# The w_down stage of a decoder layer by Strassen's seven block products

## The chip, the cores and the metric

One Trainium2 chip, one core of it. TensorE multiplies, VectorE and ScalarE work on tiles, GpSimd is nearly unused, and SyncE (SP) issues the DMA transfers. The metric is the time of one execution on the device in microseconds; before the change 788.14 (median of 3 runs, 787.05 to 790.59).

## The reference, cut to what matters

One decoder layer in float32: 512 tokens of width 1024. A normalised and modulated input goes through two attention branches, their outputs through gates and an output projection into a residual; then follows the SwiGLU block, of width 2816, that the change is about:

```python
h = rms_norm(x, g_ffn_norm[l]) * (1.0 + sc_f) + sh_f
g_ff, u_ff = jnp.split(h @ w_gate_up[l], 2, axis=-1)
x = x + gt_f * ((jax.nn.silu(g_ff) * u_ff) @ w_down[l])
```

`gt_f`, the output gate, is a row of 1024 numbers made from `c` and `w_mod`. It multiplies each output column.

## The kernel before, in words

Every large product is done in three passes (`mm3`). Each operand is split into a high part (ScalarE casts it to the fast matmul format) and a low part (VectorE subtracts the high part from the original); the passes are high x high, high x low, low x high, added up in one PSUM bank. So a weight tile passes through SP (load into one of three staging tiles `st`), ScalarE (`wh`) and VectorE (`wl`) before TensorE can use it; `wh` and `wl` have three buffers each.

The work is a list of chunks, run in order by `drive`. A chunk is 256 weight rows by 512 columns; `prep(c + 2)` is started when chunk c has begun: it takes the loaded staging tile, has it split, and issues the load of the chunk after. All other work beside the matmuls (splitting of activations, rows of gates, normalisation) is a set of generators, called tasks. A planner with a modelled clock for each engine (`Clocks`) decides while the program is written where their instructions go: `step` lets a task go on when what it yields is ready on that clock, `pump` moves TensorE's modelled clock on where something is missing, and `need_room` and `room` wait for a free buffer of a tag. Each engine then runs its instructions in the order in which they were written; nothing is reordered on the chip.

The up stage makes, for each of 11 groups `gi`, 256 features: four 128-feature blocks (two of the gate part, two of the up part) in four PSUM banks. `up_done` takes Silu of the gate part on ScalarE into a tile `s`, multiplies the up part into it on VectorE, and a task `up_split` makes high and low parts, which stay in SBUF: `g` tiles for groups 0 to 3, `K` for 4 to 7, `O` for 8 to 10. Even groups use the `acc` banks, odd ones the banks `s`, `tr`, `tr`, `pv`. The normalised input `h2` lies in the four `H` tiles.

The last stage, w_down, runs once for each half of the 1024 output columns: 11 chunks of 256 rows, for each 128-row block k and token tile i (128 tokens) one `mm3` into the bank of that token tile. Before a chunk's weights are split, `gated` multiplies them by `gt_f` on VectorE. At the end `add_store` adds the bank to the residual `x1` and SP stores the sum. In the second half `down_end` runs the last chunk's part of the last token tile in two pieces of 256 columns, each with its own bank, add and store:

```python
def gated(half):
    def change(st):
        pump(lambda: "gtf" in ready)
        ve.tensor_tensor(out=st, in0=st, in1=gtf[half].unsqueeze(1).to_broadcast([P, 2, 512]), op=ALU.mult)
```

Of the kernel before, what the change touches and what calls it, by code (L numbers as in the profile page):

```python
# [24 lines left out]
P = 128  # L26
# [87 lines left out]
def layer(ctx, tc, x, vecs, w_mod, w_in, gvecs, w_br_dsa, w_br_moba, w_out, w_gate_up, w_down, cosh, sinh, cosi, sini, out):  # L114
# [48 lines left out]
    def mm3(acc, lh, ll, rh, rl, first, last):  # L163
        te.matmul(acc, lh, rh, start=first, stop=False)
        te.matmul(acc, lh, rl, start=False, stop=False)
        te.matmul(acc, ll, rh, start=False, stop=last)
# [385 lines left out]
    def group(srcs, n, accs_of, mm, order, fin, need=(), change=None, end=None):  # L552

        accs = {}
        nk = 2 * len(srcs)
        chunks = []
        for c, src in enumerate(srcs):
            def unit(w, ks, js, last, c=c):
                if not accs:
                    accs.update(accs_of())  # L560

                held_back[0] = 1.0 if last else 0.0
                pieces = [(k, j) for j in js for k in ks] if last else [(k, j) for k in ks for j in js]
                if end and last and js[-1] == order[-1]:
                    del pieces[-len(ks):]
                for a, b in pieces:

                    full = nk - 2 if end and b == order[-1] else nk

                    emptied_next[0] = last and a == ks[-1]  # L570
                    mm(accs[b], w[0][:, a], w[1][:, a], 2 * c + a, b, c == 0 and a == 0, 2 * c + a == full - 1)
                    if end and b == order[-1] and 2 * c + a == full - 1:
                        fin(b, accs[b], False)
                        done(accs[b])
# [5 lines left out]
                if end and last and js[-1] == order[-1]:  # L580
                    end(w, [2 * c + a for a in ks])
# [5 lines left out]
            chunks.append((lambda src=src, n=n: wload(src, 2, n), units, need, change))  # L587
        return chunks

    def drive(chunks, ws, ahead=2):  # L590
# [6 lines left out]

        def prep(c):
            if c < len(chunks) and chunks[c][0]:
                yield lambda: 0.0 if c in sts else None  # L600
                st = sts.pop(c)
                if chunks[c][3]:
                    chunks[c][3](st)
                yield st
                uid[0] += 1
                h, l = [wp.tile(list(st.shape), F32R, name=f"w{q}_{uid[0]}", tag="w" + q) for q in "hl"]
                se.copy(h, st)
                yield h
                ve.tensor_tensor(out=l, in0=st, in1=h.bitcast(F32), op=ALU.subtract)
                done(st)  # L610
                ws[c] = h, l
            load(c + 1)

        load(ahead)
        for c, (load_of, units, need, _) in enumerate(chunks):
            pump(lambda: all(f in ready for f in need) and (not load_of or c in ws))
            for u, unit in enumerate(units):
                unit(ws.get(c))
                if u == 0:
                    spawn(prep(c + ahead), slack=4.0, rank=-1, on=(DVE,))  # L620
                    step()
            ws.pop(c, None)
# [604 lines left out]
    act = []  # L1227

    def up_split(src, hi, lo):
        f = f"act{len(act)}"  # L1230
        act.append((hi, lo))
        yield src
        se.copy(hi, src)
        yield hi
        ve.tensor_tensor(out=lo, in0=src, in1=hi.bitcast(F32), op=ALU.subtract)
        done(src)
        ready.add(f)

    def up_done(gi):
        half = {}  # L1240

        def fin(f, acc):
# [6 lines left out]
            if gi < 4:  # L1249
                need_room("g")  # L1250
                need_room("g")
                dst = t("g", [P, S], F32R), t("g", [P, S], F32R)
            else:
                if not f:
                    need_room("K" if gi < 8 else "O")
                    half["big"] = t("K" if gi < 8 else "O", [P, 4, S], F32R)
                dst = half["big"][:, 2 * f, :], half["big"][:, 2 * f + 1, :]
# [47 lines left out]

    gtf = []
# [12 lines left out]
    def down_mm(acc, wh, wl, k, i, first, last):  # L1319
        sl = slice(i * P, (i + 1) * P)  # L1320
        pump(lambda: f"act{k}" in ready)
        main3(acc, act[k][0][:, sl], act[k][1][:, sl], wh, wl, first, last)

    def gated(half):
        def change(st):
            pump(lambda: "gtf" in ready)
            ve.tensor_tensor(out=st, in0=st, in1=gtf[half].unsqueeze(1).to_broadcast([P, 2, 512]), op=ALU.mult)
        return change

    def add_store(i, cols, part, store=True):  # L1330
# [5 lines left out]
    def down_done(half):  # L1336
        return lambda i, acc, store=True: add_store(i, slice(half * 512, half * 512 + 512), acc, store)

    def down_end(w, ks):

        sl = slice((NT - 1) * P, NT * P)
        for a, tag in ((0, "pv"), (256, "s")):
            need_room("ps" + tag)
            part = ps(tag, (P, 256))
            cs = slice(a, a + 256)
            for n, k in enumerate(ks):
                mm3(part, act[k][0][:, sl], act[k][1][:, sl], w[0][:, n, cs], w[1][:, n, cs], n == 0, n == len(ks) - 1)
            add_store(NT - 1, slice(512 + a, 768 + a), part)
            done(part)

    for half in range(2):
        hs = slice(half * 512, half * 512 + 512)
        chunks += group([[w_down[k2 * 256:(k2 + 1) * 256, hs]] for k2 in range(NF // 2)], 512,
                        four() if half else other_four, down_mm, [0, 1, 2, 3], down_done(half), change=gated(half),
                        end=down_end if half else None)

    with tc.manual_schedule(engines=engines):
        start = max(ck.at.values())
        ck.at = {e: start for e in engines}
        free.update({tag: [start] * n for tag, n in list(NB.items()) + [("st", 3)]})  # L1360
# [23 lines left out]
        spawn(gtf_task())  # L1384
        dve = (DVE,)
# [48 lines left out]
```

## Time and profile before

| | before |
|---|---|
| median of 3 runs | 788.14 us |
| the profiled execution | 790.77 us |
| its span, first to last instruction | 788.7 us |
| mean granted TensorE clock | 0.993 |
| TensorE / VectorE / ScalarE / GpSimd busy | 780.8 / 478.3 / 363.4 / 30.4 us |
| DMA | 100.61 MB, mean 128 GB/s |

The rows come from one profiled execution. A busy TensorE is not one at its peak, since matmuls overlap: a row's mean duration of a matmul is longer than the distance to the next. What a matmul costs is read from a run of them in the chain of waits, as time over count.

### The profile page before, as it was taken

The numbers are of one execution on the slowest core, as the hardware profiler recorded it, in microseconds if no ns is written. First come the engines' busy times: TensorE is split into PE (matmuls) and PEld (weight loads), VectorE is DVE, ScalarE is ACT, GpSimd is POOL, SyncE is SP. The second block draws the span as 40 slices with busy tenths as digits, with TensorE's granted clock in tenths as the row PEclk, the third lists the DMA queues.
The fourth block names the chain that finished last, engine by engine and source line by source line (L and its number), as shares of the span: only waits on it lengthen the run. The fifth ranks groups of instructions, "written<-read, shape, count | busy, mean of one in ns | idle before, by whom it ended". The sixth has DMA issues, their size and how long they took to land.

```text
span 788.7 us, 10060 instructions
## 1 busy us (share of the span) xinstructions
PE 780.8 (99%) x3734; PEld 649.7 (82%) x3734; DVE 478.3 (61%) x876; ACT 363.4 (46%) x767; POOL 30.4 (4%) x32
## 2 busy tenths in 40 slices
PE   7999999999999999999999999999999999999998
PEld 6887888888788878888889988888888888888886
DVE  5874889989799786248777365323333334544542
ACT  5664587779776747624446132222332332211210
POOL 2000012011111000000000000000000000000000
PEclk8999999999999999999999999999999999999999
DMA  9957443542136364334520166333233232333311
GB/s 302 334 173 225 129 162 81 150 141 58 31 88 200 111 213 152 118 106 146 165 90 27 56 200 207 98 107 107 85 104 107 81 105 62 127 107 113 128 54 53
DMA packets 80156, 100.61 MB, mean 128 GB/s; under 512 B 8096, under 2 KB 48360, under 8 KB 80108
## 3 DMA queue, kind: packets, MB, share of 16 engines
q1 hardware_dynamic: 80108, 99.98, 40.7%
q8 instruction: 29, 0.48, 0.2%
q14 instruction: 19, 0.16, 0.1%
HBM read 97.86 MB, written 2.11 MB: 127 GB/s over the span
## 4 chain that ended last, share of the span: by engine, by line
PE 98%; DMA 1%; ACT 0%; SPq 0%; issue 0%; DVE 0%; ACTq 0%
PE psacc L107 64%; PE pstr L107 16%; PE pspv L107 9%; PE pss L107 9%; DMA K<-in_w_mod_dram 1%; SPq L218 0%; ACT H L107 0%; SPq L202 0%; DVE V L107 0%; ACT acol L107 0%; DVE mcol L107 0%; ACT mcol L107 0%; DVE acol L107 0%; ACTq L107 0%
## 5 line engine op out<-in xcount | busy, mean ns | idle before, releaser
L107 DVE TENSOR_TENSOR wl<-st,wh 128x1024 fp32r<-128x1024 f32 (+1 forms) x120 | 145.1, 1209 | 134.8 <-ACT wh L107 134.8
L107 ACT CAST wh<-st 128x1024 fp32r<-128x1024 f32 (+1 forms) x120 | 124.4, 1037 | 172.8 <-PE psacc L107 62.1
L107 PE MATMUL psacc<-H,wh 128*128 128x512 f32 x576 | 183.0, 399 | 0.0
L107 PE MATMUL psacc<-wh,H 128*128 128x512 f32 x384 | 127.3, 403 | 0.3 <-ACT H L107 0.2
L107 PEld LDWEIGHTS psacc<-H,wh 128*128 128x128 f32 x576 | 106.2, 188 | 22.3 <-issue 2.1
L107 PE MATMUL psacc<-H,wl 128*128 128x512 f32 x288 | 112.6, 391 | 0.0
L107 PEld LDWEIGHTS psacc<-wh,H 128*128 128x128 f32 x384 | 72.7, 190 | 16.1 <-ACT H L107 1.1
L107 PE MATMUL psacc<-wl,H 128*128 128x512 f32 x192 | 72.0, 396 | 0.0
L107 PEld LDWEIGHTS psacc<-H,wl 128*128 128x128 f32 x288 | 54.1, 188 | 11.6
L107 PE MATMUL pstr<-H,wh 128*128 128x512 f32 (+1 forms) x176 | 54.3, 390 | 0.0
L107 POOL TENSOR_TENSOR m<-m,mhalf 128x4 f32<-128x4 f32 (+1 forms) x24 | 28.6, 1191 | 394.9 <-DVE m L107 360.9
L107 PEld LDWEIGHTS psacc<-wl,H 128*128 128x128 f32 x192 | 36.8, 192 | 7.0
L107 PE MATMUL psacc<-wh,K 128*128 128x512 f32 x128 | 39.8, 390 | 0.0
L107 PE MATMUL psacc<-O,wh 128*128 128x512 f32 x128 | 39.5, 390 | 0.0
L107 PEld LDWEIGHTS pstr<-H,wh 128*128 128x128 f32 (+1 forms) x176 | 32.3, 184 | 7.6
L107 ACT ACTIVATE s<-s,att 128x256 f32<-128x256 f32 (+3 forms) x64 | 34.2, 562 | 4.0 <-DVE att L107 3.8
L107 DVE TENSOR_TENSOR s<-psacc,s 128x512 f32<-128x512 f32 x12 | 8.3, 692 | 43.7 <-PE psacc L107 43.7
L107 PE MATMUL pstr<-H,wl 128*128 128x512 f32 (+1 forms) x88 | 34.3, 390 | 0.0
L107 ACT ACTIVATE s<-psacc 128x512 f32<-128x512 f32 x12 | 7.2, 598 | 47.6 <-PE psacc L107 47.6
L107 PEld LDWEIGHTS psacc<-wh,K 128*128 128x128 f32 x128 | 24.0, 188 | 5.0
L107 PEld LDWEIGHTS psacc<-O,wh 128*128 128x128 f32 x128 | 24.0, 188 | 5.0
L107 DVE TENSOR_TENSOR st<-st,cg 128x1024 f32<-128x1024 f32 x22 | 26.8, 1219 | 0.0
(236 smaller groups left out, 1362.9 us busy)
## 6 DMA issues: line engine op xcount, KB each, us to landing
st<-in_w_gate_up_dram SPq DMA_DIRECT2D x88, 256.0 KB, 3.2
st<-in_w_in_dram SPq DMA_DIRECT2D x36, 512.0 KB, 3.6
K<-in_w_mod_dram SPq DMA_DIRECT2D x12, 1024.0 KB, 6.7
st<-in_w_down_dram SPq DMA_DIRECT2D x22, 512.0 KB, 3.6
K<-in_w_mod_dram SPq DMA_DIRECT2D x16, 512.0 KB, 6.1
st<-in_w_in_dram SPq DMA_DIRECT2D x16, 256.0 KB, 4.7
st<-in_w_mod_dram SPq DMA_DIRECT2D x8, 512.0 KB, 3.7
O<-in_x_dram SPq DMA_DIRECT2D x4, 512.0 KB, 5.3
```

What stands on the lines that cost most here:

```text
L107: inst = f(*args, **kw)
```

## The change: what it does

The last stage is computed as a 2 x 2 block product. Tokens are halved (256 each), the features of every group are halved (128-row blocks 2c and 2c + 1 of w_down), and the output columns are halved (512 each). Instead of eight block products there are seven, M1 to M7, each over 11 pairs of row blocks and two token tiles. Their operands are blocks and sums of blocks: S1 to S4 of the activations and T1 to T4 of the weights, made on VectorE in float32 before the split into high and low parts.

- After each up group a task `combine` makes S1 to S4. A11, S2, S1 and S3 stay in SBUF (`g`, `K`, `O` tiles as before). A12, A22 and S4 go, split, into an `O` tile and from there to device memory by a transfer on GpSimd's queue (`second0` to `second10`, 768 KB each).
- The stage has two halves. The first runs M1, M6, M7 and M5 for pairs 0 to 10, with B11 and T1 to T3 of each pair, from 768 KB of w_down; B11 + T3, that is T2, is also stored to device memory (256 KB, GpSimd's queue). The second runs M2, M3 and M4 with B21, B22 and T4, from 512 KB of w_down and the 256 KB stored. `second_task` loads the second activations back into `K` and `O` tiles as these come free.
- Split weights live in three sets (`homes`): one in four of the six `wh` and `wl` buffers, two in the `H` tiles, which the last up group leaves in two steps. Second blocks `b` of a load use `pT` tiles, and `gu` tiles after the last group's activations are stored. Preparation begins three chunks ahead.
- M2 goes on in M1's banks. At the first half's end `shared_sums` copies M1 and makes the sums from which three of the four output quarters start; `share` gates them and adds them to `x1`. The gate no longer multiplies weights: `settle` multiplies each product's bank by `gt_f` and then adds it.
- The last two chunks of the second half run together, product by product; the last one (M4, second token tile) takes them in two pieces of 256 columns.

```diff
         def prep(c):
+            early = c < len(chunks) and chunks[c][3]
+            def load_next():
+                if c + 1 < len(chunks) and chunks[c + 1][3]:
+                    yield room("st"), lambda: block_room()
+                load(c + 1)
             if c < len(chunks) and chunks[c][0]:
                 yield lambda: 0.0 if c in sts else None
+                if early:
+                    yield from load_next()
+                ws[c] = yield from (chunks[c][3] or split)(sts.pop(c))
+            if not early:
+                yield from load_next()
+        begun = [ahead]
+        def prepare(c):
+            while begun[0] <= c + (ahead + 1 if begun[0] < len(chunks) and chunks[begun[0]][3] else ahead):
+                spawn(prep(begun[0]), slack=4.0, rank=-1, on=(DVE,))
+                begun[0] += 1
...
+    def combine(gi, a0, a1):
+        first, other = slice(0, 256), slice(256, 512)
+        yield a0, a1, room("gu", 2)
+        s13, s4 = t("gu", [P, 2, 256]), t("gu", [P, 256])
+        ve.tensor_tensor(out=s13[:, 0], in0=a0[:, other], in1=a1[:, other], op=ALU.add)
+        ve.tensor_tensor(out=s13[:, 1], in0=a0[:, first], in1=a0[:, other], op=ALU.subtract)
+        ve.tensor_tensor(out=a0[:, other], in0=s13[:, 0], in1=a0[:, first], op=ALU.subtract)
+        ve.tensor_tensor(out=s4, in0=a1[:, first], in1=a0[:, other], op=ALU.subtract)
+        if gi < 4:
...
+        va = a0.rearrange("p (a d) -> p a d", a=2)
+        se.copy(ha, va)
+        se.copy(hb, s13)
+        yield ha, hb
+        ve.tensor_tensor(out=la, in0=va, in1=ha.bitcast(F32), op=ALU.subtract)
+        ve.tensor_tensor(out=lb, in0=s13, in1=hb.bitcast(F32), op=ALU.subtract)
+        done(a0, s13)
...
+        yield s4, a1, room("O")
+        v1 = a1.rearrange("p (a d) -> p a d", a=2)
+        x = t("O", [P, 6, 256], F32R)
+        se.copy(x[:, 0:2], v1)
+        se.copy(x[:, 2], s4)
+        yield x
+        ve.tensor_tensor(out=x[:, 3:5], in0=v1, in1=x[:, 0:2].bitcast(F32), op=ALU.subtract)
+        ve.tensor_tensor(out=x[:, 5], in0=s4, in1=x[:, 2].bitcast(F32), op=ALU.subtract)
+        done(a1, s4)
+        second_acts[gi] = dp.tile([P, 6, 256], F32R, name=f"second{gi}")
+        pool_dma(second_acts[gi], x, out_of=x)
+        done(x)
+        ready.add(f"stored{gi}")
...
             ve.tensor_tensor(out=half[f], in0=acc, in1=half[f], op=ALU.mult)
-            spawn(up_split(half[f], *dst), rank=0)
-            step()
-            if gi == 0 and f:
+            if f and not gi:
                 done(*w0_tiles)
                 ready.add("ffn0")
+            if f:
+                spawn(combine(gi, half[0], half[1]), rank=0)
+            if f and gi == NF // 2 - 1:
+                done(h2[1], h2[3])
+            step()
...
+    last_up = chunks[-2][1]
+    last_up[0] = lambda w, unit=last_up[0]: (done(h2[0], h2[2]), unit(w))
...
+    def homes(n):
+        sets[0] += 1
+        uid[0] += 1
+        if sets[0] % 3 == 1:
+            yield room("W")
+            parts = [wp.tile([P, 2, 512], F32R, name=f"w{q}{m}_{uid[0]}", tag="w" + q) for m in range(2) for q in "hl"]
+            taken("W", parts[0])
+            return [(parts[0], parts[1]), (parts[2], parts[3])], parts[:1]
+        yield room("H", 2)
+        h, l = t("H", [P, n, 512], F32R), t("H", [P, n, 512], F32R)
+        return [(h[:, 0:2], l[:, 0:2]), (h[:, 2:], l[:, 2:])], (h, l)
...
+    def split_into(places, blocks):
+        yield tuple(b for b, _ in blocks)
+        for (b, view), (h, l) in zip(blocks, places):
+            se.copy(h, view)
+        yield tuple(h for h, _ in places)
+        for (b, view), (h, l) in zip(blocks, places):
+            ve.tensor_tensor(out=l, in0=view, in1=h.bitcast(F32), op=ALU.subtract)
...
+    def block_tag():
+        tags = [tag for tag in ("pT", "gu") if free[tag] and (tag == "pT" or f"stored{NPAIR - 1}" in ready)]
+        return min(tags, key=lambda tag: min(free[tag]), default=None)
...
+    def load_first_half(c):
+        st, b = rows_of(2 * c), t(block_tag(), [P, 512])
+        last_dma[0] = nc.sync.dma_start(b, w_down[(2 * c + 1) * P:(2 * c + 2) * P, 512:])
+        arriving(b, 512)
+        return c, st, b
+    def split_first_half(loaded):
+        c, st, b = loaded
+        yield st, b, room("s")
+        t2 = t("s", [P, 512])
+        ve.tensor_tensor(out=b, in0=b, in1=st[:, 1], op=ALU.subtract)
+        ve.tensor_tensor(out=t2, in0=b, in1=st[:, 0], op=ALU.add)
+        ve.tensor_tensor(out=st[:, 1], in0=st[:, 1], in1=st[:, 0], op=ALU.subtract)
+        sums2[c] = dp.tile([P, 512], F32, name=f"sums{c}")
+        places, tiles = yield from homes(4)
+        (h0, l0), (h1, l1) = places
+        places = [(h0, l0), (h1[:, 0], l1[:, 0]), (h1[:, 1], l1[:, 1])]
+        yield from split_into(places, [(st, st), (b, b), (t2, t2)])
+        pool_dma(sums2[c], t2, out_of=t2)
+        done(st, b, t2)
+        return {"B11": (h0[:, 0], l0[:, 0]), "T1": (h0[:, 1], l0[:, 1]), "T3": places[1], "T2": places[2]}, tiles
...
+    def load_second_half(c):
+        st, b = rows_of(2 * c + 1), t(block_tag(), [P, 512])
...
+    def split_second_half(loaded):
+        c, st, b = loaded
+        yield st, b
+        ve.tensor_tensor(out=b, in0=st[:, 0], in1=b, op=ALU.subtract)
+        places, tiles = yield from homes(3)
+        (h0, l0), (h1, l1) = places
+        places = [(h0, l0), (h1[:, 0], l1[:, 0])]
+        yield from split_into(places, [(st, st), (b, b)])
+        done(st, b)
+        return {"B21": (h0[:, 0], l0[:, 0]), "B22": (h0[:, 1], l0[:, 1]), "T4": places[1]}, tiles
...
+    def second_task():
+        for q in range(NPAIR):
+            yield (f"stored{NPAIR - 1}", "down",
+                   lambda: min([min(free[tag]) for tag in ("K", "O") if free[tag]], default=None))
+            tag = min((tag for tag in ("K", "O") if free[tag]), key=lambda tag: min(free[tag]))
+            x = t(tag, [P, 6, 256], F32R)
+            pool_dma(x, second_acts[q])
...
+    def settle(i, half, acc, cs=slice(0, 512), store=True):
+        pump(lambda: "gtf" in ready)
+        need_room("s")
+        tmp = t("s", [P, 512])
+        n = cs.stop - cs.start
+        ve.tensor_tensor(out=tmp[:, :n], in0=acc[:, :n], in1=gtf[half][:, cs], op=ALU.mult)
+        cols = slice(half * 512 + cs.start, half * 512 + cs.stop)
         xs = x1[i // 2][:, i % 2, cols]
-        ve.tensor_tensor(out=xs, in0=xs, in1=part, op=ALU.add)
+        ve.tensor_tensor(out=xs, in0=xs, in1=tmp[:, :n], op=ALU.add)
+        done(tmp)
         if store:
             nc.sync.dma_start(ov[:, i, cols], xs)
...
+    def shared_sums(n, tt, acc):
+        if n == "M1":
+            kept["M1", tt] = fresh()
+            se.copy(kept["M1", tt], acc)
+        elif n == "M6":
+            kept["U2", tt] = fresh()
+            ve.tensor_tensor(out=kept["U2", tt], in0=acc, in1=kept["M1", tt], op=ALU.add)
+            done(kept["M1", tt])
+        elif n == "M7":
+            kept["U3", tt] = fresh()
+            ve.tensor_tensor(out=kept["U3", tt], in0=acc, in1=kept["U2", tt], op=ALU.add)
+        else:
+            c22, c12 = fresh(), fresh()
+            ve.tensor_tensor(out=c12, in0=acc, in1=kept["U2", tt], op=ALU.add)
+            ve.tensor_tensor(out=c22, in0=acc, in1=kept["U3", tt], op=ALU.add)
+            done(kept["U2", tt])
+            spawn(share(tt, c12, c22, kept["U3", tt]), slack=1.0, rank=3, on=(DVE,))
+    def share(tt, c12, c22, u3):
+        yield "gtf"
+        for i, half, c in ((2 + tt, 1, c22), (tt, 1, c12), (2 + tt, 0, u3)):
+            yield c
+            ve.tensor_tensor(out=c, in0=c, in1=gtf[half], op=ALU.mult)
...
+            ve.tensor_tensor(out=xs, in0=xs, in1=c, op=ALU.add)
+            done(c)
+            if c is c22:
+                nc.sync.dma_start(ov[:, i, 512:], xs)
...
+    first_half = [("M1", "A11", "B11", ("tr", "tr")), ("M6", "S2", "T2", ("pv", "s")),
+                  ("M7", "S3", "T3", ("acc", "acc")), ("M5", "S1", "T1", ("acc", "acc"))]
+    second_half = [("M2", "A12", "B21", None), ("M3", "S4", "B22", ("pv", "s")), ("M4", "A22", "T4", ("acc", "acc"))]
...
+        def part(w, rows):
+            begin(w)
+            held_back[0] = 0.0 if second or c < last else 1.0
+            for n, a, b, tags in rows:
+                for tt in range(2):
...
+                    ends = c == last if not second else c == last - 2 and (n, tt) == ("M4", 1)
+                    product(n, a, b, tt, c, held, ends, acc, start=not c and n != "M2", skip=n == "M2")
+                    if ends:
+                        emptied_next[0] = False
+                        finish(n, tt)
+                        step()
+            if rows[-1] is table[-1]:
+                leave(c)
+        def end(w):
+            begin(w)
+            held_back[0] = 1.0
+            for n, a, b, tags in table:
+                for tt in range(2):
+                    if (n, tt) == ("M4", 1):
+                        continue
+                    for q in (last - 1, last):
+                        emptied_next[0] = q == last
+                        product(n, a, b, tt, q, held, q == last, banks[n, tt], skip=n == "M2")
+                    emptied_next[0] = False
+                    finish(n, tt)
+                    step()
+            n, a, b, _ = table[-1]
+            for e, tag in ((0, "pv"), (256, "s")):
+                need_room("ps" + tag)
+                acc = ps(tag, (P, 256))
+                cs = slice(e, e + 256)
+                for q in (last - 1, last):
+                    product(n, a, b, 1, q, held, q == last, acc, cs=cs, start=q != last, more=False)
+                settle(3, 0, acc, cs=cs)
+                done(acc)
+            leave(last - 1, last)
+        return [lambda w: part(w, table[:2]), lambda w: part(w, table[2:])]
```

## Rows read from the trace of the kernel before

**Rows 1.** The page's busy shares and granted clock in 40 slices.

```profile
PE 780.8 (99%) x3734; PEld 649.7 (82%) x3734; DVE 478.3 (61%) x876; ACT 363.4 (46%) x767; POOL 30.4 (4%) x32
...
PEclk8999999999999999999999999999999999999999
```

**Rows 2.** The page's chain of waits, shares of the span by engine.

```profile
PE 98%; DMA 1%; ACT 0%; SPq 0%; issue 0%; DVE 0%; ACTq 0%
```

**Rows 3.** Windows: stretch, each engine's busy us (instructions), clock, DMA share, GB/s.

```profile
443.70:643.70 200.00, 200.00 (x898) 166.22 (x897) 81.05 (x93) 59.66 (x77) 0.00 (x0) 1.00 0.38 116
...
665.60:725.60 60.00, 60.00 (x267) 49.71 (x266) 29.75 (x28) 12.83 (x14) 0.00 (x0) 1.00 0.33 106
725.60:785.60 60.00, 59.98 (x271) 49.76 (x269) 26.25 (x25) 9.85 (x10) 0.00 (x0) 1.00 0.23 79
```

**Rows 4.** Chain of waits from 720 us: start, us, engine, tile.

```profile
725.67 58.48 PE psacc L107 x258
784.15 0.71 PE pspv L107 x6
784.86 0.73 PE pss L107 x6
785.62 0.42 DVE V L107
```

**Rows 5.** VectorE's groups by shape from 665.6 us: count, busy us, mean ns, idle.

```profile
L107 DVE TENSOR_TENSOR wl<-st,wh 128x1024 fp32r<-128x1024 f32 x21 | 25.7, 1225 | 47.4 <-ACT wh L107 47.4
L107 DVE TENSOR_TENSOR st<-st,cg 128x1024 f32<-128x1024 f32 x20 | 24.4, 1219 | 0.0
...
L107 DVE TENSOR_TENSOR O<-s,O 128x512 fp32r<-128x512 f32 x2 | 1.4, 683 | 0.0
```

**Rows 6.** VectorE's timeline, 663 to 673 us: start, duration, idle before.

```profile
663.22 0.69 DVE L107 TENSOR_TENSOR s<-psacc,s 128x512 f32<-128x512 f32 x1 [6.10 <-PE psacc L107]
663.83 1.22 DVE L107 TENSOR_TENSOR st<-st,cg 128x1024 f32<-128x1024 f32 x1
...
667.14 1.22 DVE L107 TENSOR_TENSOR wl<-st,wh 128x1024 fp32r<-128x1024 f32 x1
668.28 0.69 DVE L107 TENSOR_TENSOR O<-s,O 128x512 fp32r<-128x512 f32 x1
668.88 1.22 DVE L107 TENSOR_TENSOR st<-st,cg 128x1024 f32<-128x1024 f32 x1
671.29 1.22 DVE L107 TENSOR_TENSOR wl<-st,wh 128x1024 fp32r<-128x1024 f32 x1 [1.19 <-ACT wh L107]
672.44 1.22 DVE L107 TENSOR_TENSOR st<-st,cg 128x1024 f32<-128x1024 f32 x1
```

**Rows 7.** ScalarE's timeline, 654 to 667 us.

```profile
654.80 1.05 ACT L107 CAST wh<-st 128x1024 fp32r<-128x1024 f32 x1 [4.39 <-PE psacc L107]
661.79 0.60 ACT L107 ACTIVATE s<-psacc 128x512 f32<-128x512 f32 x1 [5.93 <-PE psacc L107]
...
666.66 0.62 ACT L107 CAST O<-s 128x512 fp32r<-128x512 f32 x1
```

**Rows 8.** DMA issues (us to landing); two busy windows, the last columns share, GB/s.

```profile
st<-in_w_down_dram SPq DMA_DIRECT2D x22, 512.0 KB, 3.6
...
20.00:40.00 20.00, 19.82 (x93) 16.27 (x92) 17.26 (x35) 13.63 (x26) 0.00 (x0) 0.92 1.08 333
460.00:480.00 20.00, 20.00 (x90) 16.54 (x89) 12.11 (x16) 6.33 (x9) 0.00 (x0) 1.00 0.64 202
```

**Rows 9.** VectorE's timeline at the end.

```profile
784.19 0.69 DVE L107 TENSOR_TENSOR V<-V,psacc 128x512 f32<-128x512 f32 x1 [0.67 <-PE psacc L107]
784.90 0.42 DVE L107 TENSOR_TENSOR V<-V,pspv 128x256 f32<-128x256 f32 x1
```

**Rows 10.** GpSimd's timeline, its last instruction.

```profile
425.38 0.55 POOL L107 TENSOR_TENSOR m<-m,mhalf 128x1 f32<-128x1 f32 x1 [5.13 <-DVE m L107]
```

**Rows 11.** VectorE's groups by shape from 430 us, one with one tensor input.

```profile
L107 DVE TENSOR_SCALAR cg<-st,cs 128x512 f32<-128x512 f32 x2 | 1.0, 477 | 0.0
```

More of the change, by code (lines that the diff above doesn't have):

```diff
@@ L550, in main3, with group @@
             step()
-    def group(srcs, n, accs_of, mm, order, fin, need=(), change=None, end=None):
+    def group(srcs, n, accs_of, mm, order, fin, need=()):
         accs = {}
@@ L563, in unit @@
                 pieces = [(k, j) for j in js for k in ks] if last else [(k, j) for k in ks for j in js]
-                if end and last and js[-1] == order[-1]:
-                    del pieces[-len(ks):]
                 for a, b in pieces:
-                    full = nk - 2 if end and b == order[-1] else nk
                     emptied_next[0] = last and a == ks[-1]
[L571 to L574, printed above, removed]
+                    mm(accs[b], w[0][:, a], w[1][:, a], 2 * c + a, b, c == 0 and a == 0, 2 * c + a == nk - 1)
                     if emptied_next[0]:
@@ L1224, in layer, with pool_dma @@
     chunks.append((None, out_units(), (), None))
[L1227 to L1237, printed above, removed]
+    pairs, pair_tiles, second_acts = {}, {}, {}
+    def pool_dma(dst, src, out_of=None):
+        nc.gpsimd.dma_start(dst, src)
+        pool = mybir.EngineType.Pool
+        tile = out_of if out_of is not None else dst
+        name = tile.tensor.name
+        at = max(ck.at.get(pool, 0.0), ck.ready.get(name, (0.0, None))[0], ck.last.get(name, (0.0, None))[0]) + 0.6
+        ck.at[pool] = at
+        landed = max(at, min(ck.dma + 1.0, at + 3.5)) + 2.6
+        if out_of is None:
+            ck.ready[name] = (landed, None)
+        ck.last[name] = (landed, None)
@@ L1317, in layer @@
     ov = out.rearrange("o (t p) d -> p (o t) d", p=P)
[L1319 to L1330, printed above, removed]
+    NPAIR = NF // 2
@@ new lines, in second_task @@
+    def second_task():
[5 more added lines that the diff above has]
+            pool_dma(x, second_acts[q])
+            pairs[q] = {n: (x[:, a], x[:, 3 + a]) for a, n in enumerate(("A12", "A22", "S4"))}
+            pair_tiles[q] = [x]
+            ready.add(f"second{q}")
@@ L1333, in add_store @@
         if store:
             nc.sync.dma_start(ov[:, i, cols], xs)
[L1336 to L1355, printed above, removed]
+    kept = {}
+    def fresh():
+        need_room("g")
+        return t("g", [P, 512])
+    def shared_sums(n, tt, acc):
[9 more added lines that the diff above has]
+            ve.tensor_tensor(out=kept["U3", tt], in0=acc, in1=kept["U2", tt], op=ALU.add)
+        else:
+            c22, c12 = fresh(), fresh()
[3 more added lines that the diff above has]
+            spawn(share(tt, c12, c22, kept["U3", tt]), slack=1.0, rank=3, on=(DVE,))
@@ new lines, in layer, with product @@
+    banks = {}
+    first_half = [("M1", "A11", "B11", ("tr", "tr")), ("M6", "S2", "T2", ("pv", "s")),
+                  ("M7", "S3", "T3", ("acc", "acc")), ("M5", "S1", "T1", ("acc", "acc"))]
+    second_half = [("M2", "A12", "B21", None), ("M3", "S4", "B22", ("pv", "s")), ("M4", "A22", "T4", ("acc", "acc"))]
+    held = {}
+    def product(n, a, b, tt, c, w, stop, acc, cs=slice(0, 512), start=False, more=True, skip=False):
+        (ah, al), (bh, bl) = pairs[c][a], w[c][0][b]
+        sl = slice(tt * P, (tt + 1) * P)
+        f = main3 if more else mm3
+        f(acc, ah[:, sl], al[:, sl], bh[:, cs], bl[:, cs], start, stop, skip)
@@ L1357, in layer @@
+    for second, load_of, split_of in ((False, load_first_half, split_first_half), (True, load_second_half, split_second_half)):
+        for c in range(NPAIR):
+            chunks.append((lambda c=c, load_of=load_of: load_of(c), down_units(c, second), (), split_of))
     with tc.manual_schedule(engines=engines):
@@ L1384, in layer @@
         spawn(gtf_task())
+        spawn(second_task())
         dve = (DVE,)
```

119 lines of the change are left out of this document (87 added, 32 removed).

## The prediction

> **What bounds the kernel now.** The page's busy line comes first: TensorE is busy 99% of the span, VectorE 61%, ScalarE 46%, GpSimd 4%, and the granted clock stands at the full 2.4 GHz level from the third slice on [rows 1]. Busy matmuls overlap, so the chain of waits is the next view: 98% of the path to the end is TensorE, with next to no waiting between its pieces [rows 2]. Then the windows by stage: from 443.7 us, where the up projection runs, to 785.6 us every microsecond holds a matmul at clock 1.00, while VectorE has 44 to 50% and ScalarE 16 to 21% of the w_down stage [rows 3]. So this stage costs what its matmuls cost, and only work beside it that grows past the matmuls can change that. The reader is to see in the chain's last rows the pace: 258 matmuls of 512 columns take 58.48 us, 0.2267 us each, and six of 256 columns 0.71 us, 0.12 each. VectorE's last add starts 0.03 us behind the last matmul and takes 0.42 [rows 4].
>
> **Term 1, matmuls removed.** Before: 22 row blocks x 4 token tiles x 2 halves x 3 passes = 528 (six of them cut into twelve of half width). After: 11 pairs x 7 products x 2 token tiles x 3 = 462, with the same six cut in two. 66 x 0.2267 = **-14.96 us**, all on the path [rows 3, 4]. The stage falls from 119.9 to 104.9 us: first half 11 chunks of 24 matmuls (5.44 us each, 59.8 in all), second half 11 of 18 (4.08, 44.9).
>
> **Term 2, what prepares a chunk, beside the matmuls.** VectorE now, per 256 rows of one column half: a gate multiply of 1219 ns and a subtraction of 1225 [rows 5]. After, in the first half: three sums of 512, a subtraction of 1024 and two of 512. One of 512 takes 0.69 us, but the next operation starts 0.61 us behind it; of 1024, 1.14 [rows 5, 6]. Two sums hang on the one before, so I take 0.69 for them: 0.69 + 0.69 + 0.61 + 1.14 + 2 x 0.61 = 4.35 us against 5.44. In the second half: 0.61 + 1.14 + 0.61 = 2.4 against 4.08. ScalarE's casts (1.05, and 0.62 for 512 [rows 7]) come to 2.3 and 1.7. Both fit. The order matters more than the load. Where the kernel of before is short of time it works one chunk after the other: multiply, 0.1 us, cast, subtract, one chunk in 3.55 us, VectorE idle 1.19 of it [rows 6]. In that pattern a new first-half chunk costs 1.99 (sums) + 0.1 + 1.05 (first cast) + 1.14 + 1.22 = 5.5 us: about the 5.44 of the matmuls, so even without overlap the loss is 0.1 us a chunk, at most 1 us. In steady state three homes for split weights exist; a home comes free two chunks ahead of its use (10.9 us, later 8.2), and casts and subtractions need about 4.
>
> **Term 3, the change-over**, where I expect the loss. It lies at 725.67 - 264 x 0.2267 = 665.8 us, and the last up group's chunks of 24 matmuls end at 654.9, 660.4 and there. Chunk 0 goes into two more of the three rotating weight buffers. ScalarE's cast at 654.80 waited for TensorE to leave such a buffer [rows 7]; now one cast waits for the last up group's second chunk and one for its third (660.4), with ScalarE's queue behind them: the first Silu of that group (661.79 today) and chunk 1's casts. With two casts and two subtractions of 512 behind that, chunk 0 is split at about 662.7, three microseconds early. Chunk 1 can go into the first normalised-input tiles, free since 654.9, but its preparation first waits for a tile for chunk 2's second block, and until the last activations are stored there are only two such tiles: chunk 0's comes free at 662.7. So chunk 1: 662.7 + the group's multiply 0.6 + 5.5 = 668.8, needed at 671.2. Chunk 2: issued at 662.7, landed after 3.6 us for 512 KB [rows 8] plus about 0.8 for its 256 KB (an estimate at the rate below), done at 668.8 + 0.6 + 5.5 = 674.9, needed at 676.7. Chunk 3: its tile comes free at 668.8; done by 674.9 + 5.5 = 680.4, needed at 682.1. Into the 1.7 us that are left must go the last group's combine: four sums of 256 (0.42 [rows 9]), three subtractions of 512 and one of 256, 3.9 us of VectorE, part of it in the gaps while casts run. So chunk 2 or 3 is late by up to 2.3 us; bounds of this term: 0 (combine fits the gaps) and 6 us (the combine ahead of the sums each time, and the loads of chunks 2 and 3 no longer hidden). I take **+1.5 us**. If a chunk is late, TensorE waits; VectorE is what is late next.
>
> **Term 4, the tail.** Today one add of 0.42 us follows the last half-width group. Now each is followed by a multiply and an add, and the tile before (the product's first token tile) still occupies VectorE for two operations of 0.69. From that tile's end T: multiply and add to T+1.4; the first half's two, T+2.2; the second half's two, T+3.0. TensorE ends at T+1.44, so VectorE lags by 1.5 us where it lags by 0.45 [rows 4, 9]. **+1.0 us** (bounds 0.4, one operation more, and 1.2). The store behind it stays.
>
> **Costed at nothing.** The change-over of the halves: four sums of TensorE's results per token tile, and the gate's multiply and add three times per token tile are 20 operations, 12 us of VectorE, in a second half that leaves it 1.6 us free per chunk, 18 in all; the bank that M2 goes on in is copied some 3 us ahead. The last two chunks run as one, so the last one's weights must be there a chunk early: its home comes free 4.08 us before, cast and subtractions need 1.05 + 1.14 + 0.61 + 0.2 = 3.0; a miss would cost a microsecond or less. In the up stage each group of 21.8 us gets four sums and a little splitting on a VectorE that is 41% busy [rows 3]. GpSimd's queue gets 33 transfers and has nothing else after 425 us [rows 10]: 11 stores of sums, 11 stores and 11 loads of activations. An activation load is issued at least 28 us ahead of its use.
>
> **DMA.** No row shows transfers from GpSimd's queue, so they are bound by volume: weights 11 x 1.5 MB (17.3), sums out 2.9, activations back 8.7, 28.9 MB, of which 2.4 MB land ahead: 26.5 MB in the 95 us to the last split. Rows with a known share give the capacity: 333 GB/s at a share of 1.08, 202 at 0.64, 106 at 0.33: 308 to 321 [rows 3, 8]. At 315, 84 us: it fits. From chunk 4 to 10 the demand is 1.84 MB per 5.44 us, 337 GB/s, a little over capacity; activations lag, with 28 us to spare. Cost 0 to 3 us, taken 0.
>
> On the Trainium skill's side, "SBUF — State Buffer", section "SBUF: two separate sides", warns that a transfer issued from GpSimd has its descriptors written by GpSimd, which VectorE locks out while a one-input operation uses both of its ports; by it transfers from that queue start late. Rows here bear on it only indirectly: an operation with one tensor input took 477 ns for 512 columns, one with two in SBUF 683 [rows 5, 11], and what the change adds on VectorE has two inputs throughout, so by that rule little would be locked out and the sum would stay.
>
> **Sum.** 790.77 - 14.96 + 1.5 + 1.0 = 778.3 us for the profiled execution (span 788.7 plus 2.07 around it). That execution stands 2.6 us over the median of the runs; the same -12.46 on 788.14 gives **775.7 us**. With the bounds of terms 3 and 4 and of the DMA: 773.6 to 784.
>
> **Rivals.** *The change-over costs most of its bound* (for it: two tiles for second blocks, VectorE with 16 us of work in 16 us; against it: the sums of a later chunk can run while casts run): +4 to +8, 778.5 to 783, about 780.5. *DMA queues up in part* (for it: 337 GB/s asked for; against it: three chunks of lead): weight chunks 4 to 10 come 1 us late each once the lead is used, +7: 783. *The other side: the 16 DMA engines set the stage's pace* (for it: mixed reads and writes from two queues are in no row; against it: shares add up to 305 to 333 GB/s everywhere). 26.5 MB in 95 us needs 279 GB/s; below that each GB/s costs time, and at 247 (107.5 us) the whole gain is gone. At 230 it takes 115 us: +20, 796. A GpSimd queue that is held up ends here too: its 22 transfers of this stage decide from 4.3 us each (95/22), and at 5.2 give the same +20. *That the products don't shrink* has no support: the counts follow from the loops.
>
> **Chances.** Forecast (773 to 778.4) 0.58; dear change-over 0.20; partial DMA queue 0.10, half of it inside the same-band; DMA-bound 0.11; below 773, 0.01. A measurement of this kernel tells about 0.5%, 3.9 us, from no change, so faster means under 784.2: 0.58 + 0.20 + 0.05 = 0.83; same 0.06; slower 0.11. A range of 773 to 784 leaves out 0.18.
>
> **What would show it.** Right: 462-matmul stage with TensorE busy in all but 1 to 3 us of it, the gap sitting 5 to 16 us behind the last up matmul and released by VectorE's low parts; the last TensorE piece to VectorE's end 1.5 us. Wrong: gaps in each chunk released by a DMA (weights, or the second activations), a DMA share near 1 through the stage, a granted clock below the full level there, or stalls already in the up stage, from stores that hold a tile.

## The result, and the profile after

The changed kernel takes 780.07 us (median of 4 runs, 779.20 to 780.84) against 787.87 for the kernel before on the same chip (4 runs, 787.05 to 790.59). The ratio is 0.9895, with a 95% interval of 0.9868 to 0.9922: 7.8 us faster, inside the range, 4.4 us behind the forecast of 775.7. The profiled execution took 780.61 us, with a span of 778.8.

From the page of the changed kernel: its busy line, the share of the chain of waits by engine, and GpSimd's DMA queue (packets, MB, share). They answer to [rows 1, 2].

```profile
PE 764.0 (98%) x3668; PEld 633.6 (81%) x3668; DVE 542.8 (70%) x1023; ACT 390.8 (50%) x824; POOL 48.2 (6%) x65
PE 93%; DVE 2%; SPq 2%; DMA 1%; issue 1%; ACT 0%; ACTq 0%; DVEq 0%
...
q0 software_dynamic: 4048, 20.19, 7.7%
```

TensorE has 3668 matmuls, 66 fewer than before, as counted. VectorE rose by 64.5 us without becoming the bound, and GpSimd's queue moved 20 MB. But the chain gives TensorE 93% where it had 98: there are waits now that weren't there. TensorE's waits name them (line, releaser: us in total, times, longest); what lies in the first 60 us, where the kernel before waits too, is left out.

```profile
PE pstr L110 <- DVE H L110: 2.2, 1, 2.2
PE pstr L110 <- DVE cg L110: 1.7, 1, 1.7
...
PE pstr L110 <- DVE gu L110: 0.7, 1, 0.7
```

The first lies in the change-over, where the prediction had put a loss. The other two lie in the up stage, which it had costed at nothing. The windows show the stages (start:end, length, busy time of PE, PEld, DVE, ACT and POOL with their instructions, granted clock, DMA share, GB/s), for comparison with [rows 3].

```profile
443.70:643.70 200.00, 197.53 (x871) 162.84 (x870) 102.92 (x147) 64.66 (x92) 4.97 (x9) 1.00 0.49 152
...
680.00:725.60 45.60, 45.60 (x199) 37.65 (x198) 35.67 (x50) 17.53 (x25) 7.52 (x14) 0.98 0.93 323
676.30:678.40 2.10, 0.00 (x0) 0.00 (x0) 2.10 (x4) 1.13 (x2) 0.91 (x2) 0.99 0.96 314
678.40:681.00 2.60, 2.58 (x6) 2.09 (x7) 2.56 (x5) 0.96 (x2) 0.00 (x0) 0.50 1.02 375
681.00:684.00 3.00, 3.00 (x13) 2.38 (x13) 2.84 (x4) 2.10 (x3) 1.08 (x2) 0.87 0.89 289
700.00:725.60 25.60, 25.60 (x115) 21.19 (x114) 17.37 (x24) 9.16 (x13) 4.29 (x8) 1.00 1.02 356
```

The reader is to see three things: the 2.5 us without a matmul in the up stage's 200 us; in the rows from 676.3 and 678.4 an empty TensorE and behind it a granted clock of 0.50, the lower of its two levels (1.2 GHz); and that from 700 us on the 16 DMA engines are full while TensorE has no gap.

**Where the time went, place by place.** One profiled execution is compared with one other. The program is the same up to the first Silu product of the up stage on VectorE. Before, it starts there at 445.87 us, after at 441.97, because the profiled execution of before had a low granted clock at its start: 0.82 in the first 20 us and 0.92 in the next, where the one after has 1.00 in both. So the stretch from that multiply to VectorE's end is the one to compare: 340.17 us before, 333.60 after, -6.6. In it:

| term | us |
|---|---|
| 66 matmuls fewer | -14.96 |
| two gaps in the up stage, start to start of the matmuls around them, less one matmul | +2.8 |
| gap ahead of chunk 2, in the same way | +2.3 |
| chunk 2's next 11 matmuls at the lower clock: 4.17 us to chunk 2's last products, against 2.63 in two experiments with the same gap and a full clock | +1.5 |
| VectorE's lag at the end, 1.61 against 0.45 | +1.2 |
| left over, not traced one by one | +0.6 |

From VectorE's end to the end of the span, with the last store, it takes 3.23 us instead of 2.66.

### The profile page after: what moved, and what is told of

Read it like the earlier page. It is cut to its first block, busy times and chain, and to the rows that moved or that the text cites. A ratio compares the mean times of both kernels' runs of the same rounds, so it can differ in the third digit from the quotient of the medians.

```text
span 778.8 us, 10322 instructions
## 1 busy us (share of the span) xinstructions
PE 764.0 (98%) x3668; PEld 633.6 (81%) x3668; DVE 542.8 (70%) x1023; ACT 390.8 (50%) x824; POOL 48.2 (6%) x65
## 4 chain that ended last, share of the span: by engine, by line
PE 93%; DVE 2%; SPq 2%; DMA 1%; issue 1%; ACT 0%; ACTq 0%; DVEq 0%
PE psacc L110 60%; PE pstr L110 15%; PE pspv L110 9%; PE pss L110 8%; SPq L183 1%; DMA K<-in_w_mod_dram 1%; DVE s L110 1%; DMA cg<-in_vecs_dram 1%; SPq L212 0%; DVE V L110 0%; DVE H L110 0%; DVE O L110 0%; ACT H L110 0%; SPq L221 0%; DVE gu L110 0%
## 5 line engine op out<-in xcount | busy, mean ns | idle before, releaser
L110 DVE TENSOR_TENSOR wl<-st,wh 128x1024 fp32r<-128x1024 f32 (+1 forms) x106 | 127.8, 1206 | 61.1 <-ACT wh L110 58.3
L110 ACT CAST wh<-st 128x1024 fp32r<-128x1024 f32 (+1 forms) x106 | 109.6, 1035 | 88.0 <-PE psacc L110 32.6
L110 PE MATMUL psacc<-H,O 128*128 128x256 f32 (+1 forms) x240 | 35.4, 305 | 0.0
L110 PEld LDWEIGHTS psacc<-H,O 128*128 128x128 f32 x240 | 32.1, 191 | 1.9
L110 ACT CAST H<-st 128x1024 fp32r<-128x1024 f32 x14 | 14.8, 1055 | 34.7 <-PE psacc L110 26.7
L110 PE MATMUL psacc<-wh,K 128*128 128x512 f32 x82 | 26.1, 389 | 0.0
```

The source lines that it names most:

```text
L110: inst = f(*args, **kw)
```

## The experiments

All runs are timed beside the kernel before on their own chip. "The stretch" is the one above, 333.60 us in the changed kernel.

**1. Another order of the homes for split weights.** The gap's own trace first: VectorE in the changed kernel (start, us, operation, out<-in, shape, idle before with its releaser).

```profile
660.01 0.69 DVE L110 TENSOR_TENSOR wl<-pT,wh 128x512 fp32r<-128x512 f32 x1 [3.79 <-ACT wh L110]
...
665.89 0.69 DVE L110 TENSOR_TENSOR s<-psacc,s 128x512 f32<-128x512 f32 x1 [2.65 <-ACT s L110]
...
673.08 0.68 DVE L110 TENSOR_TENSOR O<-s,O 128x512 fp32r<-128x512 f32 x1
...
674.89 0.42 DVE L110 TENSOR_TENSOR O<-gu,O 128x256 fp32r<-128x256 f32 x1
675.22 0.68 DVE L110 TENSOR_TENSOR pT<-pT,st 128x512 f32<-128x512 f32 x1
...
677.15 1.22 DVE L110 TENSOR_TENSOR H<-st,H 128x1024 fp32r<-128x1024 f32 x1
```

ScalarE, with the casts that these operations waited for,

```profile
659.36 0.62 ACT L110 CAST wh<-pT 128x512 fp32r<-128x512 f32 x1 [4.40 <-PE psacc L110]
...
673.24 1.06 ACT L110 CAST H<-st 128x1024 fp32r<-128x1024 f32 x1 [0.47 <-issue]
```

and TensorE there:

```profile
675.87 0.39 PE L110 MATMUL pstr<-H,g 128*128 128x512 f32 x1
678.42 2.50 PE L110 MATMUL pstr<-H,g 128*128 128x512 f32 x5 [2.17 <-DVE H L110]
...
682.59 2.91 PE L110 MATMUL psacc<-H,g 128*128 128x512 f32 x12
```

Chunk 2's high parts were cast from 673.24 on, its subtraction could have run at 674.3; it stands behind the last group's four subtractions and chunk 3's three sums in VectorE's queue. The reason lies 15 us earlier: VectorE idles 3.79 us for the cast of chunk 0, whose rotating weight buffer TensorE had not left, and 2.65 us for the first Silu of the last group, which stands behind the casts of chunks 0 and 1 on ScalarE. The edit gives chunk 0 the first pair of `H` tiles and chunk 1 the rotating set.

```diff
-        if sets[0] % 3 == 1:
+        if sets[0] % 3 == 2:
```

> One digit changed: the first chunk of the last stage goes into two tiles of the normalised input (free two up chunks before the change-over) and the second into the rotating weight buffers, instead of the other way round. Theory (order on VectorE's queue): in the changed kernel VectorE stood idle 3.8 + 2.65 us between 656 and 666 us behind casts that waited for TensorE to leave a weight buffer, and then was 2.15 us late with chunk 2. With the homes swapped the first split runs in that idle time; the gap of 2.15 us in front of chunk 2 shrinks to under 0.5 and with it goes the stretch at half clock behind it: 3.5 to 4.3 us less than the changed kernel, 776 to 776.6. Rival (transfers are late: the share of the DMA engines is 1.0 from 676 us): the gap stays within 0.5 us of 2.15, since no transfer is issued earlier for chunk 2's first block: 780.

Measured: 775.86 us (775.40 to 777.49), ratio 0.9851 (0.9821 to 0.988). The gap is gone and no other took its place: chunk 2's subtraction starts 2.3 us ahead of the matmul that needs it (the second of the six below, at 675.69), and the matmuls run on. VectorE and then TensorE of this kernel:

```profile
673.39 1.22 DVE L110 TENSOR_TENSOR H<-st,H 128x1024 fp32r<-128x1024 f32 x1
```

```profile
675.46 1.52 PE L110 MATMUL pstr<-H,g 128*128 128x512 f32 x6
```

The stretch is 329.03 us, 4.6 shorter: 2.3 of the gap, 1.5 of the clock behind it, 0.3 from a shorter first gap in the up stage, and 0.5 that is not traced. The gap went without any transfer made smaller, so the rival, that late transfers cause it, falls.

**2. The up stage's gaps: tell the planner that the bias row arrives later.** VectorE and then TensorE in the changed kernel, around both of them:

```profile
486.22 0.68 DVE L110 TENSOR_TENSOR gu<-cg,gu 128x512 fp32r<-128x512 f32 x1
...
491.17 0.69 DVE L110 TENSOR_TENSOR cg<-pstr,cg 128x512 f32<-128x512 f32 x1 [2.53 <-DMA cg<-in_vecs_dram]
```

```profile
486.96 0.50 PE L110 MATMUL pstr<-gu,oner 128*128 128x512 f32 x1 [0.74 <-DVE gu L110]
...
488.66 0.62 PE L110 MATMUL pss<-H,wh 128*128 128x512 f32 x2
...
491.92 0.73 PE L110 MATMUL pstr<-H,wh 128*128 128x512 f32 x2 [1.74 <-DVE cg L110]
```

A row of the output gate is summed by two matmuls into a `tr` bank. The first gap lies between these two: the second needs the row's low part, which VectorE makes only at 486.22, behind a weight subtraction. Then VectorE adds a bias, and it can do so 4.2 us after the bias load's issue (486.93 to 491.17), where the planner reckons with 2.7. While VectorE waits, the bank is taken, and the odd up group that begins at 488.66 wants it: the second gap. Before the change VectorE waited for the same load nearly as long, but the two matmuls stood 5.3 us ahead of the next odd group, with matmuls of the even group, on the `acc` banks, in between; the bank was free again at 487.99, and TensorE lost nothing. VectorE and TensorE of the kernel before:

```profile
487.30 0.69 DVE L107 TENSOR_TENSOR cg<-pstr,cg 128x512 f32<-128x512 f32 x1 [2.36 <-DMA cg<-in_vecs_dram]
```

```profile
486.33 0.63 PE L107 MATMUL pstr<-gu,oner 128*128 128x512 f32 x2
...
491.59 0.62 PE L107 MATMUL pss<-H,wh 128*128 128x512 f32 x2
```

With the change the first of the two matmuls stands 2.8 us ahead of the odd group, and the add ends 3.2 us behind that group's start. That it was the new work of `combine` that moved this task is argued from the planner's working; no run shows it by itself. The edit adds 2.5 us to the modelled arrival, so that the planner keeps the bank free meanwhile:

```diff
         arriving(acc, 512)
+        if tag == "st":
+            ck.ready[acc.tensor.name] = (ck.ready[acc.tensor.name][0] + 2.5, None)
```

> The planner's arrival time for the gate's bias row is set 2.5 us later (4.1 us measured from issue, the planner reckons with 2.7), so the gate's two matmuls and its add are written later in the queues; no instruction is added or taken away. Theory: the two gaps of TensorE near 487 and 491 us (0.74 + 1.74 us) come from the bank that the gate's sums hold while VectorE waits for that row; the second one goes, and 1.5 to 2.5 us with it: 777.6 to 778.6. Rival (the stores on GpSimd's queue slow the row's transfer, so it is late wherever it is planned): a gap of the same size stays: 780.

Measured: 776.70 us (775.84 to 777.23), ratio 0.9857 (0.9833 to 0.988). Both gaps are gone. That the gain was larger than expected has a reason in the rows, at least for the profiled execution: the gap ahead of chunk 2 is still there at its full size, but in this execution the clock did not fall behind it (TensorE, then a window).

```profile
675.22 1.42 PE L110 MATMUL pstr<-H,g 128*128 128x512 f32 x5 [2.21 <-DVE H L110]
676.48 0.85 PE L110 MATMUL pspv<-H,g 128*128 128x512 f32 x3
```

```profile
676.00:678.30 2.30, 2.30 (x11) 1.88 (x10) 2.27 (x5) 0.15 (x1) 0.00 (x0) 1.00 0.99 352
```

The five matmuls behind the gap take 1.26 us to the next ones, in the changed kernel 2.30. The stretch is 329.03, 4.6 shorter: 2.8 of the gaps and 1.5 of the clock come to 4.3.

**3. Matmuls of zeros in the gap.** If the price of the gap is partly the clock, work of no use there gives that part back and the gap's length stays. `zeror` is a tile of zeros; the lines that make it are left out here.

```diff
+            if not second and c == 2 and rows[0][0] == "M1":
+                for _ in range(9):
+                    te.matmul(banks["M5", 1], zeror, identr.unsqueeze(1).to_broadcast([P, 4, P]), start=False, stop=False)
```

> Nine matmuls of a zero tile (they add zero to a bank, 9 x 0.227 = 2.04 us) are put in front of chunk 2, where TensorE stood idle for 2.15 us. Theory of the clock: the idle time itself stays paid, but the stretch at 0.50 granted clock from 678.4 to 681 us (and 0.87 to 684) goes, worth 1.5 to 2.1 us: 778 to 778.6. Rival: the clock falls all the same, or matmuls there run slow for another reason (weights or transfers at the same time): 780 or later.

Measured: 779.22 us (778.29 to 781.68), ratio 0.9895 (0.9866 to 0.9924). The clock stays at 1.00 and the stretch is 332.09, 1.5 shorter, the price read above. The medians, 0.85 us apart, lie inside each other's spread, so the times can't tell it. Nor does the one trace show that the zeros held the clock: in experiments 2 and 6 it held behind the same gap without them. What stands is the price, from executions with and without the fall.

**4. Only a sixth of the second activations loaded.** If transfers set any of the stage's pace, loads of 128 KB instead of 768 KB shorten it. The kernel leaves out the rest: all second products read the one part that is loaded.

```diff
-            pool_dma(x, second_acts[q])
-            pairs[q] = {n: (x[:, a], x[:, 3 + a]) for a, n in enumerate(("A12", "A22", "S4"))}
+            pool_dma(x[:, 0], second_acts[q][:, 0])
+            pairs[q] = {n: (x[:, 0], x[:, 0]) for n in ("A12", "A22", "S4")}
```

> The eleven loads of the second activations bring a sixth of their bytes (128 KB for 768 KB), and the second half's products all read that one part; the output's values are left wrong by it, the instructions on the engines stay. Theory: transfers are hidden, TensorE's gap in front of chunk 2 and the stage's length stay within 0.5 us, time 779.5 to 780.6. Rival (the DMA engines, at a share of 0.93 to 1.0 from 676 to 726 us, take part in the loss): 2 us or more come back.

Measured: 780.32 us (778.86 to 783.05), ratio 0.9897 (0.9872 to 0.9923): the changed kernel's time. The windows of this kernel and, below, of the changed one show that less was moved and nothing won:

```profile
690.00:726.00 36.00, 36.00 (x160) 29.81 (x160) 27.73 (x39) 12.34 (x18) 5.38 (x10) 1.00 0.71 228
```

```profile
690.00:725.60 35.60, 35.60 (x159) 29.48 (x158) 27.27 (x38) 13.34 (x19) 5.89 (x11) 1.00 0.92 316
```

From its first matmul to its last the stage takes 109.3 us here and 109.2 in the changed kernel. The stretch of this execution, 335.37 us, is 1.8 longer for another reason: the granted clock fell a second time, behind the second gap of the up stage (1.82 us here). From 493.9 to 497.3 us it is 0.50, with 9 matmuls, where the changed kernel has 17 at 1.00.

**5. Both mended** (the edits of 1 and 2 together).

> Both repairs together: homes swapped, and the bias row's arrival planned 2.5 us later. If the two losses are separate, as the theory has it, they add: 4.2 us (775.86 against 780.07) and the 2.5 us of the two gaps in the up projection, 773.0 to 774 against 787.75 of before; TensorE has no gap from 443 us to its last matmul, which lies 104.7 to 105.2 us behind the first of the last stage. Rival (one delay only moves the other, VectorE being full near the change-over): a gap of 1 us or more comes up in a new place, 775 or later.

Measured: 774.50 us (772.64 to 774.86), against 786.92; ratio 0.9831 (0.9817 to 0.9844). It beats both kernels, and its windows have a matmul in every microsecond from the up stage to the end, at clock 1.00:

```profile
443.70:643.70 200.00, 200.00 (x888) 165.68 (x887) 104.74 (x152) 65.99 (x94) 4.97 (x9) 1.00 0.48 154
663.20:680.00 16.80, 16.80 (x76) 13.91 (x75) 16.56 (x28) 8.25 (x13) 2.69 (x5) 1.00 0.69 226
680.00:725.00 45.00, 45.00 (x200) 37.28 (x199) 35.21 (x50) 18.20 (x26) 6.96 (x13) 1.00 0.92 314
725.00:768.00 43.00, 43.00 (x197) 35.76 (x195) 37.80 (x54) 12.79 (x16) 1.58 (x3) 1.00 0.62 228
```

The stretch is 326.36, 13.8 us under that of before: the 14.96 of the removed matmuls less 1.2 of VectorE's lag. The 0.6 left over in the table went with the gaps. So the gaps and what followed them are all that the changed kernel lost of its gain, apart from the tail.

**6. The tail without the gate** on the last two pieces of 256 columns.

```diff
-        ve.tensor_tensor(out=tmp[:, :n], in0=acc[:, :n], in1=gtf[half][:, cs], op=ALU.mult)
...
-        ve.tensor_tensor(out=xs, in0=xs, in1=tmp[:, :n], op=ALU.add)
+        if n < 512:
+            ve.tensor_tensor(out=xs, in0=xs, in1=acc[:, :n], op=ALU.add)
+        else:
+            ve.tensor_tensor(out=tmp[:, :n], in0=acc[:, :n], in1=gtf[half][:, cs], op=ALU.mult)
+            ve.tensor_tensor(out=xs, in0=xs, in1=tmp[:, :n], op=ALU.add)
```

> The changed kernel with the gate's multiply left out for the last two pieces of 256 columns (their output is left ungated). Theory: in the tail VectorE runs four operations of about 0.43 us where two would do and ends 1.61 us behind TensorE; without the two multiplies it ends 0.7 to 0.9 us behind, and the time is 0.7 to 0.9 us less, about 779.2. Rival (the store behind it sets the end whatever VectorE does): no change, 780.

VectorE's end in the changed kernel, with two operations for each piece, and then in this one, with one:

```profile
773.91 0.42 DVE L110 TENSOR_TENSOR s<-pspv,cg 128x256 f32<-128x256 f32 x1
774.36 0.43 DVE L110 TENSOR_TENSOR V<-V,s 128x256 f32<-128x256 f32 x1
774.70 0.42 DVE L110 TENSOR_TENSOR s<-pss,cg 128x256 f32<-128x256 f32 x1
775.15 0.42 DVE L110 TENSOR_TENSOR V<-V,s 128x256 f32<-128x256 f32 x1
```

```profile
773.56 0.41 DVE L110 TENSOR_TENSOR V<-V,pspv 128x256 f32<-128x256 f32 x1
773.89 0.41 DVE L110 TENSOR_TENSOR V<-V,pss 128x256 f32<-128x256 f32 x1
```

The matmuls end at 773.96 and 773.61, so the lag falls from 1.61 to 0.69 us. The time is 779.54 us (776.68 to 780.54), ratio 0.9897 (0.9878 to 0.9916): 0.9 us is less than these runs tell apart. In this execution too the clock held behind the 2.21 us gap, and the stretch of 331.3 is 0.9 + 1.5 us below the changed kernel's, within 0.1.

**7. Each load of second activations made twice**, to see how near the transfers are to the bound.

```diff
             pool_dma(x, second_acts[q])
+            pool_dma(x, second_acts[q])
```

> Each of the eleven loads of the second activations is made twice, 8.7 MB more in the last stage. By the capacity that I reckoned with ahead (315 GB/s) some 35 MB need 111 us where 95 are there: about 16 us more than the changed kernel, 796. By the 375 GB/s that the changed kernel's rows show at a share of 1.0 they need 94 us: under 3 us more, 780 to 783, with gaps only where a second load comes too late. Theory that GpSimd's queue itself is slow (its own work for each load): gaps in front of second-half chunks, released by these loads, whatever the share.

Measured: 803.41 us (801.08 and 805.74), ratio 1.0206 (1.0174 to 1.0238). TensorE's new waits, GpSimd's, and two windows of the second half:

```profile
PE pstr L110 <- DMA K<-second: 8.2, 2, 5.7
PE pstr L110 <- DMA O<-second: 6.1, 3, 3.0
PE pstr L110 <- ACT wh L110: 2.4, 1, 2.4
```

```profile
POOL K L1245 <- DMA K<-second: 44.6, 6, 11.3
POOL O L1245 <- DMA O<-second: 36.7, 5, 8.5
```

```profile
740.00:760.00 20.00, 15.39 (x60) 11.93 (x58) 17.21 (x25) 6.37 (x8) 2.11 (x4) 0.91 1.04 384
760.00:790.00 30.00, 17.89 (x60) 13.41 (x61) 6.88 (x9) 3.14 (x4) 3.69 (x7) 0.78 0.65 222
```

Neither figure that I had worked out from volume holds. From 740 to 760 us TensorE idles 4.6 us while the DMA engines are full, so bytes may have a part there; but most of its idle time, 12.1 us, comes from 760 to 790 us, where they stand at 0.65, and the lower clock (0.78) adds to it. GpSimd issues each second load only when the first into the same tile has landed: it waits 81 us in all, and the loads behind wait too. That wait is made by the doubling; it doesn't show that the queue was near a limit in the changed kernel. What volume alone the stage would bear stays open.

## Why the prediction was right, and where it was off

**Term 1** held: in experiment 5 the stage runs from 663.19 to 768.1 us, the 104.9 predicted, and its stretch accounts for all 66 matmuls.

**Term 2** held: no chunk but the third waited for its preparation, with VectorE at 78% in 680 to 725.6 us.

**Term 3** had the right place, victim and releaser: chunk 2 late by the low parts, "up to 2.3 us", measured 2.17 idle and 2.3 start to start. I took 1.5, a size without a row behind it, where my own walk had named 2.3. What the term lacked is the clock: the lower level that followed the gap cost another 1.5 us in this execution. The mechanism was partly another: I had counted the last group's combine against the free time of VectorE; what decided was the order of the queue, where chunk 2's subtraction stood behind chunk 3's sums, and the 6.4 us that VectorE had idled for ScalarE just before (experiment 1). The tile for second blocks that I had made the gate of chunk 1 came free as I had said, with chunk 0's split, but at 660.7 us instead of 662.7: SP issued chunk 2's block into it at 660.73, and VectorE began chunk 1's sums at 661.22. Whether chunk 1 waited for that tile or only stood behind chunk 0's subtractions in VectorE's queue, no run separates.

**Term 4**: a lag of 1.5 us forecast, 1.61 measured; experiment 6 shows 0.9 of it to be the gate's multiplies. What follows VectorE's end, taken as unchanged, is 0.6 us longer; this has not been traced further.

**Costed at nothing** is where the prediction failed: "in the up stage each group of 21.8 us gets four sums and a little splitting on a VectorE that is 41% busy". The share was read rightly, and even after the change it is 51%, but it was the wrong thing to look at. Other tasks were placed elsewhere in the queues, and one of them met a group that shares its bank: 2.8 us, which experiment 2 gives back by planning that one task later, with no instruction added or taken away. Half change-over and last chunks did cost nothing.

**DMA**: a capacity of 308 to 321 GB/s was too low; 356 to 375 GB/s were moved at a share of 1.02, so chunks 4 to 10, at 337 asked, were served. Experiment 4 shows the cost of 0 that I took.

**The rivals.** Dear change-over: 3.8 us with its clock, just under its 4 to 8. Partial queue and DMA-bound: neither. TensorE waited for no load in this stage; VectorE waited for loads of `w_down`, 10.9 us in seven waits of at most 3.1, and the matmuls hid that. GpSimd's queue issued each transfer in 0.54 us beside a busy VectorE; no issue in 680 to 730 us took over 0.55. By the Trainium skill, "SBUF — State Buffer", section "SBUF: two separate sides", an operation with two inputs in SBUF shuts out only a GpSimd operation that reads SBUF, so by it writing descriptors would not be held up; the 0.55 us agree, as far as an issue's duration shows it.

**In sum**: forecast -12.5, measured -7.8. Not foreseen are 2.8 us of the up stage and, where the clock falls, 1.5; undersized by 0.8 is the gap. With the 0.6 left over, 0.6 behind VectorE's end and 0.2 of the lag this comes to -6.0, what the stretch and the time behind it give in the two profiled executions. The medians give 1.8 more; the time ahead of the stretch alone differs by 2.1 us among the profiled executions with the change (441.26 to 443.39), and the clock doesn't always fall. That the time still lies in the range is in part luck: the up stage was in no bound, and the room came from the bounds of the change-over and the DMA. Experiment 5 has no gap; by my terms without one it should gain 14.0. Its stretch gives 13.8, of which the longer time behind VectorE's end takes 0.7, and its medians 12.4, with an interval of 12.3 to 14.4.

## What to carry to other kernels

Where each engine runs its instructions in a fixed order, added work is priced by what it is queued ahead of, not by the free share of its engine: walk the queue at every point where buffers change hands, and ask of each task that moves which bank it now shares with whom. A gap of TensorE can cost more than its length; read the granted clock behind it. A stall from a planner's wrong arrival time can sleep in a kernel until another change moves it onto the path.

## What the hardware showed that I had not expected

A gap of 2.2 us ahead of chunk 2 occurs in five of the profiled executions (the changed kernel and experiments 2, 4, 6 and 7). The granted clock fell behind it in the changed kernel, 4 and 7, where the next 11 matmuls took 4.1 to 4.2 us, and held in 2 and 6, where they took 2.63. The up stage's second gap, 1.3 to 1.8 us long, occurs in six of them (the changed kernel and experiments 1, 3, 4, 6 and 7), and the clock fell behind it in 4 alone. What makes the difference was not settled.

With GpSimd's transfers beside them, SP's loads of `w_down` land later, 4.8 us in the median of the page against 3.6 [rows 8], and GpSimd's own of 768 KB take 5.3 (stores) to 7.5 us:

```profile
st<-in_w_down_dram SPq DMA_DIRECT2D x22, 512.0 KB, 4.8
second<-O POOLq DMA_DIRECT2D x11, 768.0 KB, 5.3
...
K<-second POOLq DMA_DIRECT2D x6, 768.0 KB, 7.5
```

The Trainium skill, "DMA: Bandwidth & Descriptors", section "Issuing engines are not separate DMA queues", says that transfers of all issuers interleave on the same 16 DMA engines; the later landings agree, and so does experiment 4, where with a sixth of those loads' bytes the loads of `w_down` land in 4.0 us.
